# One state operand per chunk for both heads, and a common place modulo 256 bytes

## The chip, the cores and the metric

The kernel runs on one core of a Trainium2 chip. The metric is device time in microseconds (us), here that of the one core. The core has a matrix engine (PE, whose weight loads the profile lists apart as PEld), a vector engine (DVE), a scalar engine (ACT), GpSimd (POOL) and a queue engine (SP) that issues most transfers. Every engine takes its own instructions in the order in which they stand.

## The reference, cut to what matters

One layer of a decoder trunk over 1024 tokens of 1024 channels: a token mixer with three branches (causal pooling, RWKV-7 time mixing, attention into 256 memory tokens), then a gated feed-forward block with a short convolution. The change lies in the RWKV-7 branch, 16 heads of 64 channels, whose core is

```python
def step(state, inp):
    rt, wt, kt, vt, an, bn = inp
    sa = jnp.einsum('bhvk,bhk->bhv', state, an)
    state = state * wt[:, :, None, :] + sa[..., None] * bn[:, :, None, :] + vt[..., None] * kt[:, :, None, :]
    yt = jnp.einsum('bhvk,bhk->bhv', state, rt)
    return state, yt
```

It starts from a zero state and gives `yt` for each of 1024 tokens. Around it stand the input projection `z = h @ w_in`, the gates, the output projections and the feed-forward products; all are float32.

## The kernel before, in words

Activations lie channel-major: 128 channels over the partitions, the tokens along the free axis. A large product is made in float32r from operands split in a high and a low part: per 128 rows of weights there are three matmuls of 128x512 (`mm3`, L167 high weights by high data, L168 high by low, L169 low by high). The projections of `h` read `hh`/`hl` as the moving side and weight tiles `whi`/`wlo` as the stationary side; POOL and ACT make `whi`/`wlo` from a raw tile.

The recurrence runs in 4 groups (`rwkv_group`), each of 4 heads: two pairs `i` of two heads, one head of a pair on partitions 0 to 63 (`lo`), the other on 64 to 127 (`up`). The tokens are cut into 16 chunks of 64. A group has three parts:

- **Chunk products** (L542 to L559), for all chunks at once: per chunk the stationary `BK` (64 rows, 128 columns: the two key-like operands of one head) meets `AR`, 128 moving columns, once for `lo` (L549) and once for `up` (L556). The banks `ps` are masked by DVE into `NT` and `AR`, and ACT copies the outputs' part to `RB`. Transposes (`pt`) and products of values (`pv`, `pbo`) stand among them.
- **Inversion** of a triangular matrix per chunk on DVE (L584 to L600), while PE works through projections (`fill_to`), then two rows of 32x32 products (`pz`, `pw`).
- **Scan** (L645 to L693), chunk after chunk. `visit` (L636) chains matmuls in an order written out: remainders `pr` (four float32 matmuls), DVE copies them to `Rs`, `pu` applies `NT`, DVE and ACT copy `pu` to `HV`, `ph` and `py` make the next state and the output, DVE adds the decayed state into `HV` of the next chunk.

[...] Matmuls with fewer than 128 rows or columns use a part of the array; the profile writes rows*columns, such as `128*64`, and two that use different columns run side by side.

A scheduler that is given the dependencies and the written-out chains sets each engine's final order and puts projection matmuls between the visits; tiles that need no certain place are laid out by pools in the order in which they are made. The program therefore fixes, for each tile, a place in its partition. Places modulo 256 bytes of the two sides of the 128x512 float32r matmuls, from the built program before (after the change both are 224 for all of these):

| moving | stationary | matmuls | which |
|---|---|---|---|
| 224 | 192 | 3776 | `hh`/`hl`, the feed-forward's first half `h2h`/`h2l`, `yh`/`yl`, `mgl` by `whi`/`wlo` |
| 64 | 192 | 640 | `oh`, `ol`, `ph_`, `pl_`, `mgh` by `whi`/`wlo` |
| 224 or 64 | 64 or 224 (unequal) | 648 | a part of `psf`, the up products with weights `wt` |
| equal | equal | 1656 | `psd` (876, `f` by `u`, both at 64), the rest of `psf` (780) |

Of the kernel before, what the change touches and what calls it, by code (L numbers as in the profile page):

```python
# [9 lines left out]
F32 = mybir.dt.float32  # L10
# [7 lines left out]
P = 128  # L18
T = 1024
# [25 lines left out]
def trunk_kernel(ctx: ExitStack, tc: tile.TileContext, xT, memT, pvec, w_in, w_kv, w_upd, w_upg,  # L45
# [59 lines left out]
                        base=-1, channel_multiplier=-1)  # L105
    G.memset(smask, 1.0)
    G.memset(smask.rearrange("p (c s) -> p c s", s=C)[:, :, 0:1], 0.0)
    eps = const.tile([P, 3], F32, name="eps")
    for j, e in enumerate((NORM_EPS, L2_EPS, LNX_EPS)):
        G.memset(eps[:, j:j + 1], e)  # L110
# [226 lines left out]

    def up_tiles():
        return (wp.tile([P, 2, P], F32, name="uraw", tag="wraw0", bufs=3),
                wp.tile([P, 2, P], FR, name="uhi", tag="uhi", bufs=2),  # L340
                wp.tile([P, P], FR, name="ulo", tag="ulo", bufs=1))

    def load_up(ap):
        raw, hi, lo = up_tiles()
        raw, hi = raw[:, 0], hi[:, 0]
        SP.dma_start(raw, ap)
        split_w(raw, hi, lo)
        return hi, lo
# [6 lines left out]
    def load_up2(ap):  # L355


        raw, hi, _ = up_tiles()
# [72 lines left out]

    def rwkv_group(g, kv):
        tagA, tagB, tagC = ([f"X{i}{(g + n) % 3}" for i in range(2)] for n in range(3))
        AR = rw.tile([P, 2, 3, T], F32, name="AR", tag="AR")
        Dc = rw.tile([P, 2, NCH], F32, name="Dc", tag="Dc")
        tBN = [rw.tile([P, 2, T], F32, name=f"tBN{i}", tag=tagC[i]) for i in range(2)]
        tHV = rw.tile([P, 2, 2, T], F32, name="tHV", tag="HV")
# [1 line left out]
        def c3(ap):  # L439
            return ap.rearrange("p (c s) -> p c s", s=C)  # L440
# [16 lines left out]
        vs = []  # L457
        turn = [0]

        def product_bank(name):  # L460

            turn[0] = (turn[0] + 1) % 3
            shape = [P, 4, 2, C]
            return pss.tile(shape, F32, name=name, tag="s") if turn[0] else \
                psk.tile(shape, F32, name=name, tag="k")

        for i in range(2):
            p = 2 * g + i
            t0_, t1_ = kv[i][:, 0], kv[i][:, 1]
            t2_, t3_ = tBN[i][:, 0], tBN[i][:, 1]  # L470
            t4_, t5_ = tHV[:, i, 0], tHV[:, i, 1]
            r_ = AR[:, i, 1]
# [12 lines left out]
            in_block(8 + p, shifted(p, r_))  # L485

            dst = c3(AR[:, i, 0])
# [51 lines left out]
        for i in range(2):  # L539
            us = slice(NCH * i, NCH * i + NCH)  # L540
            for c0 in range(0, NCH, 4):
                def bc(m, q):  # L542
                    return m[q].unsqueeze(1).broadcast_to([64, 4, C])
                cs = slice(c0, c0 + 4)
                lo, up = slice(0, 64), slice(64, 128)
                ps = product_bank("ps1")
                for c in range(4):
                    t = slice((c0 + c) * C, (c0 + c + 1) * C)
                    PE.matmul(ps[:, c], BK[i][lo, c0 + c], AR[lo, i, 0:2, t], start=True, stop=True)  # L549
                A.copy(RB[i][:, 0, cs], ps[:, :, 1])  # L550
                V.tensor_tensor(NT[lo, i, cs], ps[lo, :, 0], bc(mstrict, lo), op=ALU.mult)
                V.tensor_tensor(c3(AR[up, i, 0])[:, cs], ps[up, :, 0], bc(mstrict, up), op=ALU.mult)
                ps = product_bank("ps2")
                for c in range(4):
                    t = slice((c0 + c) * C, (c0 + c + 1) * C)
                    PE.matmul(ps[:, c], BK[i][up, c0 + c], AR[up, i, 1:3, t], start=True, stop=True)  # L556
                A.copy(RB[i][:, 1, cs], ps[:, :, 0])
                V.tensor_tensor(NT[up, i, cs], ps[up, :, 1], bc(mstrict, up), op=ALU.mult)
                V.tensor_tensor(c3(AR[lo, i, 2])[:, cs], ps[lo, :, 1], bc(mstrict, lo), op=ALU.mult)  # L559
            for b in range(2 if i == 0 else 0):  # L560
                bonus(b)

# [40 lines left out]
        for u0 in (0, 16):  # L603
# [11 lines left out]
                for q0, q1 in ends:  # L615
                    PE.matmul(ps[q0, u], Z[q1, u0 + u], NTu[q1, u0 + u, 32:64], start=True, stop=True)
            for q0, q1 in ends:
                A.copy(NTu[q0, us, 32:64], ps[q0])


        for i in range(2):
# [2 lines left out]
                                op=ALU.mult)  # L624


        lo, up = slice(0, 64), slice(64, 128)
# [4 lines left out]
        def bank(name):  # L632
            turn[0] ^= 1
            return (psc if turn[0] else psk).tile([P, 2, C], F32, name=name, tag="c" if turn[0] else "k")

        def visit(products, after):  # L636

# [8 lines left out]
        for c in range(NCH):  # L646
            t = slice(c * C, (c + 1) * C)
            once = dict(start=True, stop=True)
            pr = bank("pr")
            py = pss.tile([P, 2, C], F32, name="py", tag="s")  # L650
            ke, ko = (up, lo) if c == 0 else (slice(0, P), slice(0, P))
            row = []
            for i in range(2):
# [4 lines left out]
            made = V.tensor_copy(Rs, pr).ins  # L658
            pu = bank("pu")
            row = []  # L660
# [5 lines left out]
            visit(row, made if c else None)  # L666
# [13 lines left out]
            if c + 1 < NCH:  # L680
# [5 lines left out]
                if c + 2 < NCH:  # L686
# [6 lines left out]
            A.copy(AR[:, :, 1, t], py)  # L693

        for i in range(2):
            p = 2 * g + i
            y = AR[:, i, 1]
# [149 lines left out]
    for hd in range(4):  # L849
        for t0, _ in HALVES:  # L850
# [7 lines left out]
            for u in range(2):  # L858
                ps = psg.tile([P, 2, 256], F32, name="psco", tag="g0")
                for tt in range(2):  # L860
                    ts_ = slice((2 * u + tt) * P, (2 * u + tt + 1) * P)
                    mm3(ps[:, tt], (qh[:, ts_], ql[:, ts_]), (kh[:, hd], kl[:, hd]), True, True)
                mx = as_.tile([P, 8], F32, name="mxs", tag="mxs", bufs=2)
# [745 lines left out]
```

## Time and profile before

| what | value |
|---|---|
| median of 3 runs | 2084.89 us (2083.38 to 2085.0) |
| the profiled execution's own time | 2084.65 us |
| its span, first to last instruction | 2082.7 us |
| mean granted PE clock | 0.993 |
| PE records | 12246 |
| stretches with chunk products (first to last) | 131.4 to 843.7 us |
| stretches of the scans | 237.0 to 968.2 us |
| up products `psf` | 1508.4 to 1845.0 us |
| down products `psd` | 1848.1 to 2056.6 us |

A row of the timeline gives start and length in us, engine, line, operation, `output<-inputs`, the part of the array (`rows*columns`), the shape, and how many equal records were merged. In a dense stream the distance from one record's start to the next is what a matmul costs; its listed length also holds the time in which its end drains while the next runs.

### The profile page before, as it was taken

To read this page: it belongs to the slowest core of one execution; us is meant where nothing else is said; L and a number is where in the kernel's file an instruction comes from. 1 tells how busy PE (TensorE), PEld (TensorE's weight loads), DVE (VectorE), ACT (ScalarE), POOL (GpSimd) and SP (SyncE) were. 2 spreads that over 40 slices of the span, in tenths; PEclk is the share of its full clock that TensorE was granted. 3 is DMA by queue.
4 is the path that set the end of the run, shared out by engine and by line. 5 is a ranking of instruction groups with operands and counts; after the bars stand their busy time and mean duration, and the time that the engine had idled before them with its cause. 6 is when DMAs were issued, how large, how long until landed. Compare 5 with 4: busy or idle time off the path is not lost.

```text
span 2082.7 us, 34125 instructions
## 1 busy us (share of the span) xinstructions
PE 2026.5 (97%) x12246; PEld 1559.1 (75%) x12246; DVE 1358.2 (65%) x2167; ACT 1070.6 (51%) x2252; POOL 810.8 (39%) x917
## 2 busy tenths in 40 slices
PE   8999999999999999999999999998999999999997
PEld 5777767776778667876878878776778877777886
DVE  6567437664667357833795452769877777777798
ACT  7585348623772368434566243545443444444644
POOL 5521213121222121212122355565578888842341
PEclk9999999999999999999999999999999999999999
DMA  4312211120212021213526443634222222169766
GB/s 155 129 41 74 67 51 67 67 82 22 87 61 89 30 92 44 86 55 120 172 84 223 129 134 107 220 102 151 94 88 83 82 78 76 61 185 273 168 178 152
DMA packets 176713, 221.83 MB, mean 107 GB/s; under 512 B 16544, under 2 KB 128288, under 8 KB 176544
## 3 DMA queue, kind: packets, MB, share of 16 engines
q1 hardware_dynamic: 163616, 204.44, 30.2%
q0 software_dynamic: 11856, 14.16, 4.2%
q8 instruction: 97, 1.59, 0.3%
q10 hardware_dynamic: 1072, 1.05, 0.1%
q14 instruction: 72, 0.59, 0.1%
HBM read 170.30 MB, written 49.28 MB: 105 GB/s over the span
## 4 chain that ended last, share of the span: by engine, by line
PE 36%; DVE 5%; DMA 4%; POOL 3%; issue 2%; ACT 2%; SPq 1%; POOLq 0%; ACTq 0%; DVEq 0%
PE psg L167 6%; PE psg L169 6%; PE psg L168 6%; PE psf L169 3%; PE psf L167 3%; PE psf L168 3%; POOL wt L1027 2%; PE psd L168 2%; PE psd L169 2%; PE psd L167 2%; DMA R<-d_f 1%; POOL sm L1012 1%; DMA a<-in_w_fup 1%; ACT d L1043 1%; DMA fw<-in_w_fdn 1%
## 5 line engine op out<-in xcount | busy, mean ns | idle before, releaser
L131 POOL TENSOR_TENSOR wlo<-wraw,whi 128x256 fp32r<-128x256 f32 x472 | 410.4, 878 | 951.7 <-ACT whi L128 760.2
L167 PE MATMUL psg<-hh,whi 128*128 128x512 f32 x928 | 383.6, 413 | 2.5 <-DVE kv L314 2.5
L169 PE MATMUL psg<-hh,wlo 128*128 128x512 f32 x928 | 379.8, 409 | 0.1
L168 PE MATMUL psg<-hl,whi 128*128 128x512 f32 x928 | 378.8, 408 | 0.0
L128 ACT CAST whi<-wraw 128x256 fp32r<-128x256 f32 x472 | 182.7, 403 | 227.9 <-PE psg L168 122.1
L167 PEld LDWEIGHTS psg<-hh,whi 128*128 128x128 f32 x928 | 174.6, 188 | 46.5 <-DVE kv L314 3.8
L169 PEld LDWEIGHTS psg<-hh,wlo 128*128 128x128 f32 x928 | 174.3, 188 | 45.9 <-POOL wlo L131 5.1
L168 PEld LDWEIGHTS psg<-hl,whi 128*128 128x128 f32 x928 | 174.7, 188 | 42.9 <-issue 3.6
L1027 POOL TENSOR_TENSOR wt<-a,wt 128x256 fp32r<-128x256 f32 x136 | 133.8, 1012 | 30.8 <-ACT wt L1026 30.8
L167 PE MATMUL psd<-f,u 128*128 128x512 f32 x292 | 115.0, 394 | 5.7 <-ACT f L1347 3.4
L168 PE MATMUL psd<-f,u 128*128 128x512 f32 x292 | 115.0, 394 | 1.0 <-DVE f L1351 1.0
L169 PE MATMUL psd<-f,u 128*128 128x512 f32 x292 | 114.3, 393 | 0.4 <-DVE u L1351 0.4
L1027 POOL TENSOR_TENSOR wt<-sm,wt 128x256 fp32r<-128x256 f32 x102 | 106.8, 1067 | 14.6 <-ACT wt L1026 14.6
L169 PE MATMUL psf<-h2h,wt 128*128 128x512 f32 x272 | 108.0, 397 | 0.4 <-POOL wt L1027 0.3
L168 PE MATMUL psf<-h2l,wt 128*128 128x512 f32 x272 | 107.0, 393 | 0.0
L167 PE MATMUL psf<-h2h,wt 128*128 128x512 f32 x272 | 106.8, 393 | 0.0
L1026 ACT CAST wt<-sm 128x256 fp32r<-128x256 f32 x102 | 37.9, 404 | 128.2 <-POOL sm L1012 124.2
L1045 DVE SCALAR_TENSOR_TENSOR d<-z,pv,d 128x1023 f32<-128x1023 f32 x68 | 91.6, 1347 | 12.0 <-ACT d L1043 9.5
L169 PE MATMUL psf<-t,wt 128*128 128x512 f32 x204 | 81.3, 399 | 1.9 <-POOL wt L1027 1.9
L168 PE MATMUL psf<-t,wt 128*128 128x512 f32 x204 | 80.3, 394 | 0.0
L167 PE MATMUL psf<-t,wt 128*128 128x512 f32 x204 | 80.2, 393 | 0.0
L685 DVE TENSOR_TENSOR HV<-ph,Hd 64x128 f32<-64x128 f32 x112 | 32.3, 289 | 71.8 <-PE ph L639 47.7
(422 smaller groups left out, 4751.3 us busy)
## 6 DMA issues: line engine op xcount, KB each, us to landing
wraw<-in_w_in SPq DMA_DIRECT2D x240, 128.0 KB, 2.3
a<-in_w_fup SPq DMA_DIRECT2D x128, 128.0 KB, 2.4
d_zg<-st SPq DMA_DIRECT2D x48, 256.0 KB, 2.7
wraw<-in_w_fup SPq DMA_DIRECT2D x80, 128.0 KB, 2.4
fw<-in_w_fdn SPq DMA_DIRECT2D x33, 256.0 KB, 4.5
fraw<-d_f SPq DMA_DIRECT2D x33, 256.0 KB, 5.2
wraw<-in_w_prwkv SPq DMA_DIRECT2D x64, 128.0 KB, 2.4
wraw<-in_w_o SPq DMA_DIRECT2D x64, 128.0 KB, 2.5
```

What stands on the lines that cost most here:

```text
L128: last_whi[0] = A.copy(hi, src).ins
L131: (V if lo_on_dve[0] else G).tensor_tensor(lo, src, hi.bitcast(F32), op=ALU.subtract)
L167: first = PE.matmul(ps, wh, xh, start=start, stop=False)
L168: PE.matmul(ps, wh, xl, start=False, stop=False)
L169: last_mm[0] = PE.matmul(ps, wl, xh, start=False, stop=stop).ins
L685: ready = V.tensor_tensor(HV[q, :, c + 1, e], ph[q], Hd[q], op=ALU.add).ins
L1012: eng.tensor_tensor(out_[u], a[u], b[u], op=op)
L1026: A.copy(w[0][:, us], src[u])
L1027: last_low[0] = G.tensor_tensor(w[1][:, us], src[u], w[0][:, us].bitcast(F32), op=ALU.subtract).ins
L1043: A.activation(d, z, AF.Identity, scale=col("cw2", j), bias=col("cb", j))
L1045: V.scalar_tensor_tensor(d[:, n:], z[:, :T - n], col(cw, j), d[:, n:], op0=ALU.mult, op1=ALU.add)
```

## The change

**One operand.** `AR` keeps its size, but is now cut into `A2`, which per chunk holds two blocks of 64 columns side by side (`e` = 0, 1), and `RY`, the receptance and later the output. For the `lo` head block 0 is set and block 1 starts at zero, for the `up` head the other way round; POOL makes the zeros (L440 and L498 of the changed kernel). One matmul of 128 rows, 128 columns and 128 moving columns per chunk then gives the products of both heads, masked as before. The outputs' products (`RY`) are no longer part of it: they are matmuls of their own, 64 moving columns by the 128 columns of `BK`, one head and eight chunks per bank, chained one behind the other.

**Remainders.** `pr` is one matmul of 128x128 by 128 columns per pair instead of two of 128x64 by 64 columns; half of its output is not used. `Rs` is twice as wide. `HV` of the first chunk gets zeros so that its full height can be read. Within a chunk `pu` now stands ahead of the `py` products of the old state.

**Places.** A tile `cpad` of 32 bytes, eight `zc` instead of four, `mxs` of 32 columns instead of 8, and `ulo` moved from one pool to another shift the tiles behind them.

```diff
+    const.tile([P, 8], F32, name="cpad")
-        zc = wp.tile([P, 1], F32, name="zc", tag="zc", bufs=4)
+        zc = wp.tile([P, 1], F32, name="zc", tag="zc", bufs=8)
...
-        AR = rw.tile([P, 2, 3, T], F32, name="AR", tag="AR")
+        AR = rw.tile([P, 6 * T], F32, name="AR", tag="AR")
+        A2 = AR[:, :4 * T].rearrange("p (i c e s) -> p i c e s", i=2, e=2, s=C)
+        RY = AR[:, 4 * T:].rearrange("p (i t) -> p i t", i=2)
+        for i in range(2):
+            G.memset(A2[lo, i, :, 1], 0.0)
...
-            A.copy(AR[64:128, i, 2], AR[64:128, i, 0])
+            A.copy(A2[up, i, :, 1], A2[up, i, :, 0])
+            G.memset(A2[up, i, :, 0], 0.0)
...
-                    PE.matmul(ps[:, c], BK[i][lo, c0 + c], AR[lo, i, 0:2, t], start=True, stop=True)
-                A.copy(RB[i][:, 0, cs], ps[:, :, 1])
+                    PE.matmul(ps[:, c], BK[i][:, c0 + c], A2[:, i, c0 + c], start=True, stop=True)
...
-                    PE.matmul(ps[:, c], BK[i][up, c0 + c], AR[up, i, 1:3, t], start=True, stop=True)
-                A.copy(RB[i][:, 1, cs], ps[:, :, 0])
+            for e, q in enumerate((lo, up)):
+                for c0 in (0, 8):
+                    ps = psc.tile([P, 8, C], F32, name="ps2", tag="c") if e and c0 else \
+                        product_bank("ps2", 8, C)
+                    for c in range(8):
+                        m = PE.matmul(ps[:, c], BK[i][q, c0 + c], RY[q, i, t], start=True, stop=True)
+                        if after is not None:
+                            later(m, after)
+                        after = m.ins
+                    A.copy(RB[i][:, e, c0:c0 + 8], ps)
...
-                row.append(((pr[up, i], AR[ko, i, 2, t], HV[ko, i, c, 1]), once))
-                row.append(((pr[lo, i], AR[ke, i, 0, t], HV[ke, i, c, 0]), once))
-            visit(row, ready)
-            Rs = rw.tile([P, 2, C], F32, name="Rs", tag="Rs", bufs=1)
+            visit([((pr[:, i], A2[:, i, c], HV[:, i, c]), once) for i in range(2)], ready)
+            Rs = rw.tile([P, 2, 2, C], F32, name="Rs", tag="Rs", bufs=1)
...
+            row = [((pu[q, i], NT[q, i, c], Rs[q, i, e]), once) for i in range(2) for e, q in enumerate((lo, up))]
             for i in range(2 if c else 0):
-                row.append(((py[lo, i], HV[lo, i, c, 0], AR[lo, i, 1, t]), kw))
-                row.append(((py[up, i], HV[up, i, c, 1], AR[up, i, 1, t]), kw))
-            row += [((pu[q, i], NT[q, i, c], Rs[q, i]), once) for i in range(2) for q in (lo, up)]
+                row.append(((py[lo, i], HV[lo, i, c, 0], RY[lo, i, t]), kw))
+                row.append(((py[up, i], HV[up, i, c, 1], RY[up, i, t]), kw))
```

What this moves on PE, the engine that the prediction turns on. In the scan, one chunk of the first group before (`psg` is a projection matmul, the others are as named above; sizes are those of the output of one matmul):

```order
L639 MATMUL pr<-HV,AR 64x64 x4
L168 MATMUL psg<-hl,whi 128x512
L639 MATMUL py<-AR,HV 64x64 x4
L639 MATMUL pu<-Rs,NT 64x64 x4
L169 MATMUL psg<-hh,wlo 128x512
L167 MATMUL psg<-hh,whi 128x512
L168 MATMUL psg<-hl,whi 128x512
L169 MATMUL psg<-hh,wlo 128x512
L639 MATMUL ph<-HV,BKN_1344 64x64 x2
L639 MATMUL ph<-HV,BKN_1345 64x64 x2
L639 MATMUL py<-RB_1342,HV 64x64 x2
L639 MATMUL py<-RB_1343,HV 64x64 x2
```

and a chunk of the same group in the changed program, up to `ph` (the four `py` matmuls behind it stand as before):

```order
L652 MATMUL pr<-HV,AR 128x128 x2
L168 MATMUL psg<-hh,whi 128x512
L169 MATMUL psg<-hl,whi 128x512
L170 MATMUL psg<-hh,wlo 128x512
L652 MATMUL pu<-Rs,NT 64x64 x4
L652 MATMUL py<-AR,HV 64x64 x4
L168 MATMUL psg<-hh,whi 128x512
L169 MATMUL psg<-hl,whi 128x512
L170 MATMUL psg<-hh,wlo 128x512
L168 MATMUL psg<-hh,whi 128x512
L652 MATMUL ph<-HV,BKN_1347 64x64 x2
L652 MATMUL ph<-HV,BKN_1348 64x64 x2
```

The remainders are two full matmuls, three projection matmuls instead of one stand between them and `pu`, and `pu` has passed `py`. With the two projection matmuls behind the last `py`, which both have, a chunk now holds 9 of them instead of 7; the number in the whole program is the same.

In the chunk products of the second group, before (L549 and L556 are the two heads' products):

```order
L549 MATMUL ps_3540<-AR,BK_3174 128x128 x4
L556 MATMUL ps_3580<-AR,BK_3174 128x128
L556 MATMUL ps_3548<-AR,BK_3174 128x128 x4
L556 MATMUL ps_3580<-AR,BK_3174 128x128
L556 MATMUL ps_3564<-AR,BK_3174 128x128 x4
L556 MATMUL ps_3580<-AR,BK_3174 128x128
L168 MATMUL psg<-hl,whi 128x512
L549 MATMUL ps_3572<-AR,BK_3174 128x128 x4
L169 MATMUL psg<-hh,wlo 128x512
L549 MATMUL ps_3588<-AR,BK_3174 128x128 x4
```

and now (L554 is the product of both heads, L566 the outputs' product):

```order
L554 MATMUL ps_3548<-AR,BK_3173 128x128 x4
L170 MATMUL psg<-hh,wlo 128x512
L168 MATMUL psg<-hh,whi 128x512
L169 MATMUL psg<-hl,whi 128x512
L554 MATMUL ps_3566<-AR,BK_3173 128x128 x4
L170 MATMUL psg<-hh,wlo 128x512
L168 MATMUL psg<-hh,whi 128x512
L169 MATMUL psg<-hl,whi 128x512
L566 MATMUL ps_3575<-AR,BK_3173 128x64 x8
L566 MATMUL ps_3585<-AR,BK_3173 128x64 x8
L566 MATMUL ps_3595<-AR,BK_3173 128x64 x8
L566 MATMUL ps_3605<-AR,BK_3173 128x64 x8
```

Of 256 chunk products with 128 moving columns 128 are left, and 256 with 64 moving columns are new, in runs of 8 to 32. Counted over the whole PE order, two neighbours use the array cut in different ways 572 times before and 376 times now: of the 196 that are gone 128 lie around `pr`, 64 around the chunk products (96 before, 32 now), 4 elsewhere.

More of the change, by code (lines that the diff above doesn't have):

```diff
@@ L339, in up_tiles @@
         return (wp.tile([P, 2, P], F32, name="uraw", tag="wraw0", bufs=3),
-                wp.tile([P, 2, P], FR, name="uhi", tag="uhi", bufs=2),
-                wp.tile([P, P], FR, name="ulo", tag="ulo", bufs=1))
+                wp.tile([P, 2, P], FR, name="uhi", tag="uhi", bufs=2))
     def load_up(ap):
-        raw, hi, lo = up_tiles()
+        raw, hi = up_tiles()
         raw, hi = raw[:, 0], hi[:, 0]
+        lo = pz.tile([P, P], FR, name="ulo", tag="ulo", bufs=1)
         SP.dma_start(raw, ap)
@@ L355, in load_up2 @@
     def load_up2(ap):
-        raw, hi, _ = up_tiles()
+        raw, hi = up_tiles()
         lo = ulo2
@@ L433, in rwkv_group @@
         tagA, tagB, tagC = ([f"X{i}{(g + n) % 3}" for i in range(2)] for n in range(3))
[L434 removed]
+        AR = rw.tile([P, 6 * T], F32, name="AR", tag="AR")
+        A2 = AR[:, :4 * T].rearrange("p (i c e s) -> p i c e s", i=2, e=2, s=C)
+        RY = AR[:, 4 * T:].rearrange("p (i t) -> p i t", i=2)
+        lo, up = slice(0, 64), slice(64, 128)
+        for i in range(2):
+            G.memset(A2[lo, i, :, 1], 0.0)
         Dc = rw.tile([P, 2, NCH], F32, name="Dc", tag="Dc")
@@ L458, in rwkv_group, with product_bank @@
         turn = [0]
-        def product_bank(name):
+        def product_bank(name, *shape):
             turn[0] = (turn[0] + 1) % 3
-            shape = [P, 4, 2, C]
+            shape = [P, *shape]
             return pss.tile(shape, F32, name=name, tag="s") if turn[0] else \
@@ L471, in rwkv_group @@
             t4_, t5_ = tHV[:, i, 0], tHV[:, i, 1]
-            r_ = AR[:, i, 1]
+            r_ = RY[:, i]
             BK = BKs[i]
@@ L485, in rwkv_group @@
             in_block(8 + p, shifted(p, r_))
-            dst = c3(AR[:, i, 0])
+            dst = A2[:, i, :, 0]
             V.scalar_tensor_tensor(dst[:, :, 1:], c3(t5_)[:, :, 1:], -1.0, c3(t3_)[:, :, :C - 1],
@@ L544, in rwkv_group @@
                 cs = slice(c0, c0 + 4)
-                lo, up = slice(0, 64), slice(64, 128)
-                ps = product_bank("ps1")
+                ps = product_bank("ps1", 4, 2, C)
                 for c in range(4):
-                    t = slice((c0 + c) * C, (c0 + c + 1) * C)
-                    PE.matmul(ps[:, c], BK[i][lo, c0 + c], AR[lo, i, 0:2, t], start=True, stop=True)
-                A.copy(RB[i][:, 0, cs], ps[:, :, 1])
+                    PE.matmul(ps[:, c], BK[i][:, c0 + c], A2[:, i, c0 + c], start=True, stop=True)
                 V.tensor_tensor(NT[lo, i, cs], ps[lo, :, 0], bc(mstrict, lo), op=ALU.mult)
[L552 to L556, printed above, removed]
-                A.copy(RB[i][:, 1, cs], ps[:, :, 0])
-                V.tensor_tensor(NT[up, i, cs], ps[up, :, 1], bc(mstrict, up), op=ALU.mult)
-                V.tensor_tensor(c3(AR[lo, i, 2])[:, cs], ps[lo, :, 1], bc(mstrict, lo), op=ALU.mult)
+                V.tensor_tensor(A2[up, i, cs, 0], ps[up, :, 0], bc(mstrict, up), op=ALU.mult)
+                V.tensor_tensor(NT[up, i, cs], ps[up, :, 1], bc(mstrict, up), op=ALU.mult)
+                V.tensor_tensor(A2[lo, i, cs, 1], ps[lo, :, 1], bc(mstrict, lo), op=ALU.mult)
+            after = None
+            for e, q in enumerate((lo, up)):
[3 more added lines that the diff above has]
+                    for c in range(8):
+                        t = slice((c0 + c) * C, (c0 + c + 1) * C)
+                        m = PE.matmul(ps[:, c], BK[i][q, c0 + c], RY[q, i, t], start=True, stop=True)
[3 more added lines that the diff above has]
+                    A.copy(RB[i][:, e, c0:c0 + 8], ps)
             for b in range(2 if i == 0 else 0):
@@ L617, in rwkv_group @@
             for q0, q1 in ends:
-                A.copy(NTu[q0, us, 32:64], ps[q0])
+                solved = A.copy(NTu[q0, us, 32:64], ps[q0]).ins
         for i in range(2):
@@ L630, in rwkv_group, with bank @@
         turn = [0]
-        def bank(name):
+        def bank(name, *shape):
             turn[0] ^= 1
-            return (psc if turn[0] else psk).tile([P, 2, C], F32, name=name, tag="c" if turn[0] else "k")
+            return (psc if turn[0] else psk).tile([P, 2, *shape, C], F32, name=name, tag="c" if turn[0] else "k")
+        V.memset(HV[lo, :, 0, 0], 0.0)
+        V.memset(HV[up, :, 0, 1], 0.0)
         def visit(products, after):
@@ L648, in rwkv_group @@
             once = dict(start=True, stop=True)
-            pr = bank("pr")
+            pr = bank("pr", 2)
             py = pss.tile([P, 2, C], F32, name="py", tag="s")
-            ke, ko = (up, lo) if c == 0 else (slice(0, P), slice(0, P))
-            row = []
-            for i in range(2):
-                row.append(((pr[up, i], AR[ko, i, 2, t], HV[ko, i, c, 1]), once))
-                row.append(((pr[lo, i], AR[ke, i, 0, t], HV[ke, i, c, 0]), once))
-            visit(row, ready)
-            Rs = rw.tile([P, 2, C], F32, name="Rs", tag="Rs", bufs=1)
+            visit([((pr[:, i], A2[:, i, c], HV[:, i, c]), once) for i in range(2)], ready)
+            Rs = rw.tile([P, 2, 2, C], F32, name="Rs", tag="Rs", bufs=1)
             made = V.tensor_copy(Rs, pr).ins
             pu = bank("pu")
-            row = []
+            row = [((pu[q, i], NT[q, i, c], Rs[q, i, e]), once) for i in range(2) for e, q in enumerate((lo, up))]
             for i in range(2 if c else 0):
                 kw = dict(start=i == 0, stop=False)
-                row.append(((py[lo, i], HV[lo, i, c, 0], AR[lo, i, 1, t]), kw))
-                row.append(((py[up, i], HV[up, i, c, 1], AR[up, i, 1, t]), kw))
-            row += [((pu[q, i], NT[q, i, c], Rs[q, i]), once) for i in range(2) for q in (lo, up)]
-            visit(row, made if c else None)
+                row.append(((py[lo, i], HV[lo, i, c, 0], RY[lo, i, t]), kw))
+                row.append(((py[up, i], HV[up, i, c, 1], RY[up, i, t]), kw))
+            visit(row, made if c else solved)
             V.tensor_copy(HV[lo, :, c, 0], pu[lo])
@@ L692, in rwkv_group @@
                         A.activation(Hd[:, i], Hn[:, i], AF.Identity, scale=Dc[:, i, c + 1:c + 2])
-            A.copy(AR[:, :, 1, t], py)
+            A.copy(RY[:, :, t], py)
         for i in range(2):
             p = 2 * g + i
-            y = AR[:, i, 1]
+            y = RY[:, i]
             gt = rw.tile([P, 2, T], F32, name="gt", tag=tagA[i])
@@ L862, in trunk_kernel @@
                     mm3(ps[:, tt], (qh[:, ts_], ql[:, ts_]), (kh[:, hd], kl[:, hd]), True, True)
-                mx = as_.tile([P, 8], F32, name="mxs", tag="mxs", bufs=2)
+                mx = as_.tile([P, 32], F32, name="mxs", tag="mxs", bufs=2)
                 V.reduce_max(mx[:, 0:2], ps, axis=AX.X)
```

1 line of the change is left out of this document (removed).

## The prediction

> **What bounds the kernel now.** I read the page first, then PE's waits.
>
> ```profile
> PE 2026.5 (97%) x12246; PEld 1559.1 (75%) x12246; DVE 1358.2 (65%) x2167; ACT 1070.6 (51%) x2252; POOL 810.8 (39%) x917
> PEclk9999999999999999999999999999999999999999
> PE psn L1096 <- DVE s L1091: 8.3, 1, 8.3
> PE psf L169 <- POOL wt L1027: 2.3, 9, 0.4
> PE pr L639 <- DVE HV L685: 0.3, 1, 0.3
> ```
>
> PE is busy 97% of the span at a full granted clock, and its longest wait for another engine is 8.3 us. So the time is what PE's records cost, one behind the other, and I cost the change in distances from start to start on PE. The last row, one wait for `HV` in 64 chunks, will prove too kind. One chunk of the first scan, from PE's timeline, and behind it the group of all late `py`:
>
> ```profile
> 253.63 0.45 PE L639 MATMUL pr<-HV,AR 128*64 128x64 f32 x8
> 254.01 0.49 PE L167 MATMUL psg<-hh,whi 128*128 128x512 f32 x1
> 254.44 0.45 PE L639 MATMUL py<-AR,HV 64*64 64x64 f32 x8
> 254.72 0.40 PE L639 MATMUL pu<-Rs,NT 64*64 64x64 f32 x8
> 255.05 0.50 PE L168 MATMUL psg<-hl,whi 128*128 128x512 f32 x1
> 255.38 0.39 PE L169 MATMUL psg<-hh,wlo 128*128 128x512 f32 x1
> 255.61 0.40 PE L167 MATMUL psg<-hh,whi 128*128 128x512 f32 x1
> 255.85 0.39 PE L168 MATMUL psg<-hl,whi 128*128 128x512 f32 x1
> 256.17 0.45 PE L639 MATMUL ph<-HV,BKN 128*64 128x64 f32 x8
> 256.45 0.40 PE L639 MATMUL py<-RB,HV 128*64 128x64 f32 x8
> 256.78 0.50 PE L169 MATMUL psg<-hh,wlo 128*128 128x512 f32 x1
> 257.12 0.40 PE L167 MATMUL psg<-hh,whi 128*128 128x512 f32 x1
> 257.49 0.45 PE L639 MATMUL pr<-HV,AR 128*64 128x64 f32 x8
> L639 PE MATMUL py<-RB,HV x512: 221/222/271, 248.8 to 968.2; 128*64 128x64 f32 x171
> ```
>
> The reader is to see that a matmul of the full array takes 0.23 us beside its like (255.38 to 255.61), but 0.32 to 0.43 where a neighbour cuts the array in another way. Eight `py` records last 0.40 us together and one lasts 0.222; two run side by side, so three steps of pairs take 0.178: 0.059 us a pair. The chunk takes 257.49 - 253.63 = 3.86 us: 7 projection matmuls at 0.233 (below) are 1.63, 20 pairs 1.18, and 1.05 is left for 6 changes of cut, 0.174 us each.
>
> **Term 1, places.** Two dense streams of one shape, each with its first and last row (210 and 466 steps), and two products of 12 matmuls out of one stage:
>
> ```profile
> 407.33 0.40 PE L169 MATMUL psg<-hh,wlo 128*128 128x512 f32 x1
> 456.33 0.39 PE L169 MATMUL psg<-hh,wlo 128*128 128x512 f32 x1
> 1925.26 0.40 PE L169 MATMUL psd<-f,u 128*128 128x512 f32 x1
> 2030.91 0.39 PE L167 MATMUL psd<-f,u 128*128 128x512 f32 x1
> 1519.62 0.39 PE L167 MATMUL psf<-t,wt 128*128 128x512 f32 x1
> 1522.11 0.39 PE L169 MATMUL psf<-t,wt 128*128 128x512 f32 x1
> 1525.71 0.39 PE L167 MATMUL psf<-h2h,wt 128*128 128x512 f32 x1
> 1528.28 0.39 PE L169 MATMUL psf<-h2h,wt 128*128 128x512 f32 x1
> ```
>
> `psg` (places 224 and 192) takes 49.00/210 = 233.3 ns, `psd` (64 and 64) 105.65/466 = 226.7. That could be the stage. But inside one stage the same two values stand side by side: the product at 1519.62 has both sides at 224 and takes 2.49/11 = 226 ns, the one at 1525.71 has moving 224 and weights 64 and takes 2.57/11 = 234. So the distance goes with the relative place, and I take it as the cause. Afterwards all places are equal. 3776 + 648 unequal matmuls at 6.6 ns are 29.2 us; the 640 with 64 against 192, whose streams I did not find dense, I take at 5 ns, 3.2 us. Together 32, the upper bound of the gain; the lower is 0, if the stage sets it. Not all arrives: half of the 4.3 us in `psf` goes into the waits for POOL's `wt`, some 1 us lies in the shadow of the 8.3 us wait, 2 more under short waits at the start and between groups. I take **-27 us**; nothing in these rows lets it be a loss.
>
> **Term 2, the scan.** `pr` becomes 4 records with 128 weight and 128 moving columns. Their price is at least a pair's 0.059 us; the nearest row is the chunk product with as many columns on both sides, 0.112 us a record (next part), and I take that. `pr` then costs 0.448 instead of 4 x 0.059 = 0.236, +0.21 us, and two changes of cut go, -0.35: -0.14 us a chunk, -8.9 in 64 chunks, and 4 changes elsewhere -0.7. On PE alone -9.6 us (-23 at 0.059).
>
> But `pr` is bound to DVE. The state behind the `ph` above, the remainders behind the last `pr` above, and a copy of 512 columns:
>
> ```profile
> 256.74 0.61 DVE L685 TENSOR_TENSOR HV<-ph,Hd 64x128 f32<-64x128 f32 x2 [1.29 <-ACT whi L128]
> 257.98 0.29 DVE L658 COPY Rs<-pr 128x128 f32<-128x128 f32 x1 [0.31 <-PE pr L639]
> L1116 DVE COPY o<-psg x16: 678/692/694, 1250.2 to 1384.0; 128x512 f32<-128x512 f32 x16
> ```
>
> `HV` is complete at 257.35, and `pr` starts 0.14 us later, at 257.49, as closely as one engine follows another here. So `pr` waits for `HV` already, though the view of waits hardly says so: from `ph` to `pr` the chain needs 1.32 us. Afterwards PE has less to do there: 0.61 for `ph` and `py` (256.17 to 256.78), 0.34 and 0.23 for two projection matmuls, no change of cut, 1.18. So 0.14 us of waiting shows in each of the 60 chunks that have a predecessor, +8.4, and the gain in place of those two matmuls, 13 ns, is lost too, +0.8. Bounds: 0, should the projections between them cover it all, and 15, should the chain also grow by 0.1.
>
> On the other side `Rs` doubles to 256 columns: between 0.29 us (128) and 0.69 (512), by proportion 0.42. It starts when `pr` has drained (three steps 0.336, one record 0.272, 0.04 to DVE: 0.65), ends at 1.07, and `pu` can follow 0.14 later, at 1.21. PE has `pr`, three projection matmuls and a change of cut ahead of `pu`: 0.448 + 0.68 + 0.17 = 1.30. That hides it with 0.09 us to spare; with the cover gone, each 0.1 us would cost 6. `pu` ahead of the old state's `py` makes `pu` earlier, and nothing waits for that `py`. I count 1 us for chunks in which `Rs` finds DVE busy. The term: -9.6 + 8.4 + 0.8 + 1 = **+0.6 us**: what the joint remainders save on PE, PE spends waiting.
>
> **Term 3, chunk products.** PE's timeline, the groups of the chunk products and of the two loads' forms, and two loads that follow one another:
>
> ```profile
> 378.50 0.49 PE L168 MATMUL psg<-hl,whi 128*128 128x512 f32 x1
> 378.92 1.16 PE L549 MATMUL ps<-AR,BK 64*128 64x128 f32 x8
> 380.00 0.50 PE L169 MATMUL psg<-hh,wlo 128*128 128x512 f32 x1
> 382.10 0.72 PE L556 MATMUL ps<-AR,BK 64*128 64x128 f32 x5
> L549 PE MATMUL ps<-AR,BK x256: 272/272/374, 131.4 to 841.0; 64*128 64x128 f32 x128
> L549 PEld LDWEIGHTS ps<-AR,BK x256: 182/188/189, 131.4 to 840.9; 64*128 64x128 f32 x128
> L639 PEld LDWEIGHTS pu<-Rs,NT x512: 129/135/136, 241.6 to 966.9; 64*64 64x64 f32 x171
> 249.15 0.19 PEld L167 LDWEIGHTS psg<-hh,whi 128*128 128x128 f32 x1
> 249.26 0.19 PEld L168 LDWEIGHTS psg<-hl,whi 128*128 128x128 f32 x1
> ```
>
> Five records last 0.72 us and one 0.272, so 0.112 us each. A projection matmul and eight records take 1.50 us: 0.233 + 0.896, and 0.37 for two changes, 0.186 each. Before: 512 records, 57.3 us, less an estimated 5 where the two heads alternate and run side by side, and 96 changes, 17.9: 70.2 us. After: 256 records of the joint product (full array) at 0.112, 28.7; 32 changes, 6.0; and 512 records of the outputs' product with 64 moving columns. What one of these costs the trace does not show. At least 0.059 us, if the moving columns set it as in the pairs; at most 0.112, if the weights do, since these are the same 128 columns of `BK`. A load lasts 188 ns for 128 columns and 135 for 64, and the loads at 249.15 and 249.26 stand 0.11 apart although both are of the same kind: a load of 128 columns seems to hold its path for 0.11 us. I take that, 0.110: 56.3 us, together 91.0, **+21 us** (-5 at 0.059).
>
> [...]
>
> POOL gets 16 fills of 64x1024 and ACT larger copies; PE has projections to do meanwhile, and POOL is busy 39%. Without that cover a fill ahead of a joint product would cost 1.4 us by the pace of the 512 columns above, an estimate, 8 times: 11 us.
>
> **The sum:** 2084.65 - 27 + 0.6 + 21 = 2079.3, told as 2079 us. The profiled execution is 0.2 us under the median, so no correction.
>
> **Rivals.** *The outputs' products stream at 0.059 us:* 26 us less, 2053. For it, a short moving side; against it, the two loads 0.11 apart. *The place is not what sets 233 ns in the projections:* another part of the stage does, and only `psf` gains, 2 us: 2084.65 - 2 + 0.6 + 21 = 2104, slower. It decides from the point at which the projections gain under 3 ns a matmul: 11 us of gain then stand against 21.6. For it: no equal pair in the groups' stage runs undisturbed; against it, both `psf` rows. [...] *The scan's chain grows:* `Rs` of twice the width is late by a further 0.12 us, where the first load after a stall lies open: +7, 2086, no change; for it the cover of 0.09. *The scan hides its wait:* the projections move into the gap, and PE keeps its 9.6 us: 2070. That the change would not do what it says is excluded by the order and the places.
>
> **How the numbers follow.** The forecast, 2079, has 0.48, its own range 2073 to 2086 (4 us of term 1, 3 of each other). Streaming 0.10, places without effect 0.16, the longer chain 0.16, the hidden wait 0.10. A measurement tells 0.2%, 4.2 us, from no change. Faster (under 2080.7): 0.32 of the forecast, 0.10, 0.10 and 0.02 of the chain: 0.54. Same: 0.14 of the forecast, 0.07 of the chain: 0.21. Slower: 0.02, 0.07 and the 0.16 of the places: 0.25. The range is 2056 to 2095: it leaves out most of streaming and of the places, and takes in the rest.
>
> **What would show it.** A dense run of `psg` at 227 ns instead of 233 (term 1). `pr` as four records 0.112 us apart, and from `ph` to `pr` still 1.32 us, so that the chunk with nine projection matmuls takes 3.86 + 2 x 0.227 = 4.31 us less some 0.05; without the wait it would be 4.13 (term 2). Outputs' products 0.11 apart, not 0.06 (term 3). It is wrong if `psg` stays at 233 ns, if PE waits for `Rs` at `pu`, or if `ph` to `pr` shrinks.

## The result

The changed kernel is slower by 1.8%: 2120.89 us (2119.2 to 2125.47, 4 runs) against 2084.14 us, a ratio of 1.0182 with a 95% interval of 1.0171 to 1.0194. The forecast was 2079 us, with a range of 2056 to 2095. The profiled execution took 2119.66 us; its span is 2117.9 us, its mean granted clock 0.978 where the kernel before had 0.993.

The page after, first PE's share and then its granted clock in 40 slices:

```profile
PE 2057.2 (97%) x12246; PEld 1613.4 (76%) x12246; DVE 1366.6 (65%) x2175; ACT 1066.3 (50%) x2220; POOL 828.7 (39%) x933
PEclk9998999899999999899999999999999999999999
```

PE has the same number of records and the same share, and yet the span is 35 us longer. Three slices of the clock row show 8, and these lie in the chunk products of three of the four groups. Cut finer, in windows of 4 us around the first of them (columns: window, length, PE's busy time and records, granted clock, DMA share, GB/s):

```profile
156.00:160.00 4.00, 4.00 (x42) 1.00 0.11 37
160.00:164.00 4.00, 4.00 (x21) 0.50 0.00 0
164.00:168.00 4.00, 4.00 (x8) 0.50 0.00 0
168.00:172.00 4.00, 4.00 (x15) 0.72 0.28 111
172.00:176.00 4.00, 4.00 (x30) 1.00 0.37 147
184.00:188.00 4.00, 4.00 (x29) 0.91 0.02 4
188.00:192.00 4.00, 4.00 (x20) 0.50 0.00 0
```

PE is busy for all of each window, and the clock halves twice. PE's timeline of the changed kernel says under what:

```profile
155.42 9.02 PE L566 MATMUL ps<-AR,BK 64*128 64x64 f32 x64
164.37 3.78 PE L520 MATMUL pbo<-kv,bonesr 128*128 128x512 f32 x4
173.80 1.97 PE L566 MATMUL ps<-AR,BK 64*128 64x64 f32 x16
186.48 6.36 PE L566 MATMUL ps<-AR,BK 64*128 64x64 f32 x32
...
200.28 0.39 PE L168 MATMUL psg<-hh,whi 128*128 128x512 f32 x1
204.82 0.39 PE L170 MATMUL psg<-hh,wlo 128*128 128x512 f32 x1
```

The rows of L566 are the outputs' products. Every float32 matmul has left two records (x512 in the trace for these 256 matmuls, x8 for the four `pr` matmuls of a chunk before), and runs are counted in records from here on. Sixteen in a row take 1.97 us at a full clock, 0.112 us apart. Within the runs of 64 and of 32 the distance changes from 0.112 to 0.213 us and stays there to the end of the run, and what comes next pays as well (`pbo`, 0.85 us from start to start behind the run, 0.43 at a full clock later in the same stage). It is so in all four groups: a run of 64 takes 8.4 to 10.5 us where 7.2 would do, a run of 32 takes 4.0 to 6.4 where 3.6 would. The clock that was missing in the eight falls, length times the missing half, sums to 30.7 us. The kernel before has no such fall between its first and its last chunk product.

The last two rows are one of the dense streams of projections, 20 steps apart: 4.54/20 = 227 ns, where the kernel before had 233. So term 1's mechanism is there, and something else cost more than it gave.

### The profile page after: what moved, and what is told of

Same layout as the page of the kernel before. It is cut to its first block, busy times and chain, and to the rows that moved or that the text cites. A ratio compares the mean times of both kernels' runs of the same rounds, so it can differ in the third digit from the quotient of the medians.

```text
span 2117.9 us, 34184 instructions
## 1 busy us (share of the span) xinstructions
PE 2057.2 (97%) x12246; PEld 1613.4 (76%) x12246; DVE 1366.6 (65%) x2175; ACT 1066.3 (50%) x2220; POOL 828.7 (39%) x933
## 4 chain that ended last, share of the span: by engine, by line
PE 64%; DVE 11%; ACT 8%; POOL 6%; DMA 5%; issue 5%; SPq 0%; POOLq 0%; ACTq 0%; DVEq 0%
PE psg L169 13%; PE psg L168 13%; PE psg L170 13%; PE ps L566 3%; POOL wt L1034 3%; PE psd L169 2%; PE psd L168 2%; PE psd L170 2%; PE pr L652 2%; DMA a<-in_w_fup 2%; POOL sm L1019 2%; PE ps L554 2%; ACT d L1050 1%; PE py L652 1%; PE pu L652 1%
## 5 line engine op out<-in xcount | busy, mean ns | idle before, releaser
L132 POOL TENSOR_TENSOR wlo<-wraw,whi 128x256 fp32r<-128x256 f32 x472 | 418.6, 896 | 948.3 <-ACT whi L129 868.8
```

The lines of the kernel that those rows point to most:

```text
L132: (V if lo_on_dve[0] else G).tensor_tensor(lo, src, hi.bitcast(F32), op=ALU.subtract)
```

## Experiments

Theory G: the places bring their gain, the remainders nothing, and the loss is the clock, which falls while long runs of the outputs' products keep PE busy and do little. Its rivals: P, that equal places make PE denser and the clock falls for that; and, on what counts as little, the share of the time in which columns stream (G1) or the unused half of the rows and the length of the run (G2). Ratios below are against the kernel before on the same chip. Three chips were used: on the first (pads alone, 128 columns, all rows, one bank) the kernel before took 2080.4 us, on the second (the changed kernel again, the remainders, one addition, the kernel before again) 2079.1, on the third (the last two kernels) 2079.4. Times from different chips are compared by their ratios.

**The pads alone**, on the kernel before:

```diff
+    const.tile([P, 8], F32, name="cpad")
-        zc = wp.tile([P, 1], F32, name="zc", tag="zc", bufs=4)
+        zc = wp.tile([P, 1], F32, name="zc", tag="zc", bufs=8)
...
+        lo = pz.tile([P, P], FR, name="ulo", tag="ulo", bufs=1)
-                mx = as_.tile([P, 8], F32, name="mxs", tag="mxs", bufs=2)
+                mx = as_.tile([P, 32], F32, name="mxs", tag="mxs", bufs=2)
```

> The kernel before with the pads alone: all places of the 128x512 float32r matmuls at 224, chunk products and scan as before. Theory G (the loss comes from the outputs' chunk products, whose long runs let the granted clock fall to 0.50; the places do what was forecast): 2084 - 27 = 2057 us, 2052 to 2064, psg 227 ns apart, no fall of the clock in the stretch of the chunk products. Rival P (equal places make PE denser, and that brings the falls of the clock): falls to 0.50 appear in the groups, and the time is 2075 to 2090.

Measured: 2071.0 us, 0.9958 (0.9943 to 0.9973): 8.7 us faster, 5.6 to 11.9. No fall of the clock in the chunk products (granted 1.00 in 150 to 200 us), so P is out. But only a third of the forecast gain arrived. Its median is the lowest of this study.

**128 moving columns** in the outputs' products of the changed kernel, everything else as it was:

```diff
-                        m = PE.matmul(ps[:, c], BK[i][q, c0 + c], RY[q, i, t], start=True, stop=True)
+                        m = PE.matmul(ps[:, c:min(c + 2, 8)], BK[i][q, c0 + c],
+                                      RY[q, i, t.start:t.start + C * min(2, 8 - c)], start=True, stop=True)
```

> The changed kernel, with the outputs' products given 128 moving columns instead of 64 (each but the last of a bank also writes the next chunk's place, which the next product then overwrites, so the outputs stay the same). Same order, same weights, same 128x64 part of the array used per head. Theory G1 (the clock falls because 64 columns stream for too small a share of the 112 ns that the weight load takes): twice the stream at 0.112 us a record still, no falls to 0.50 in the groups, 2121 - 31 = 2090 us (2084 to 2098). Rival G2 (what counts is that half of the rows is unused, or the length of the runs): falls as before, 2115 to 2125.

**All 128 rows** in them, 64 moving columns:

```diff
-                        m = PE.matmul(ps[:, c], BK[i][q, c0 + c], RY[q, i, t], start=True, stop=True)
+                        m = PE.matmul(ps[:, c], BK[i][:, c0 + c], RY[:, i, t], start=True, stop=True)
```

> The changed kernel, with the outputs' products taken over all 128 rows instead of one head's 64, still with 64 moving columns; they then add up both heads, which changes what is computed in the outputs. Theory G1 (share of streaming): falls to 0.50 in all four groups as before, 2115 to 2125 us. Rival G2 (unused rows): no falls, about 2090.

Measured: 2089.61 us (1.0049, 1.0031 to 1.0066) and 2085.5 us (1.0026, 1.0013 to 1.0039). One row of PE's timeline and one window of each, first 128 columns, then 128 rows:

```profile
154.90 7.02 PE L566 MATMUL ps<-AR,BK 64*128 64x128 f32 x64
150.00:200.00 50.00, 49.59 (x316) 1.00 0.16 59
```

```profile
154.98 7.25 PE L566 MATMUL ps<-AR,BK 128*128 128x64 f32 x64
150.00:200.00 50.00, 50.00 (x317) 1.00 0.16 59
```

Twice the moving columns in the same run of 64, mostly at the same 0.112 us a record: no fall. Twice the rows with the short stream: no fall either, so G1 as I had put it is wrong, and so is G2. Either doubling is enough: with a record every 0.112 us, 64 rows by 64 moving columns let the clock fall, 64 by 128 and 128 by 64 do not. That the clock follows the product of rows and columns would fit, but it is not shown.

**One bank** for all outputs' products, so that each 16 records wait for ACT's copy and other matmuls come between:

```diff
-                    ps = psc.tile([P, 8, C], F32, name="ps2", tag="c") if e and c0 else \
-                        product_bank("ps2", 8, C)
+                    ps = psk.tile([P, 8, C], F32, name="ps2", tag="k")
```

> The changed kernel, with all outputs' products in one PSUM bank, so that each 16 records wait for ACT's copy and the order puts other matmuls between: runs of at most 16 of them, where there were runs of 64 and 32. Theory G (the length of a run in which PE streams little): few or no falls to 0.50, 2121 - 31 = 2090 us, up to 2100 with waits for the copies. Rival P (pads): falls stay wherever psg is dense, 2115 to 2125.

Measured: 2093.59 us, 1.0070 (1.0054 to 1.0087), no fall in the groups' chunk products. One window, with the busy time of PE, PEld, DVE, ACT and POOL ahead of the clock:

```profile
150.00:200.00 50.00, 50.00 (x327) 41.81 (x322) 34.54 (x71) 28.45 (x62) 5.96 (x8) 1.00 0.18 64
```

With the records as they were and their runs cut, the loss goes too. How long a run it takes can be worked out from the records of the clock. Within a trace all its changes lie on one grid with a step of 3.41 us. In the changed kernel (both profiled executions) and in this one, each of the 16 falls in the chunk products came at the end of a step in which the outputs' products had 0.72 to 1.00 of the time. Every other step there that began at a full clock had 0.67 or less, and the clock stayed at 1.00 behind it.

**The changed kernel again**, beside the others:

> The changed kernel itself, beside the others on one chip. Theory G: falls of the clock to 0.50 in all four groups, some 30 us above the kernel with 128 moving columns (about 2118 where the kernel before takes 2080).

Measured: 2116.9 us, 1.0181 (1.0164 to 1.0198), with falls in all four groups. Against the kernel with 128 columns that is 1.0181 - 1.0049 = 0.0132, 27.5 us, between 22 and 33 by the two intervals. This is what the falls cost, since at a full clock the records are 0.112 us apart in both kernels. The clock missing in the falls of this profile sums to 35.8 us, where it was 30.7 in the first: how long a fall lasts changes from execution to execution, and not all of it lengthens the kernel.

**The remainders as before**, on the kernel with 128 moving columns:

```diff
-            pr = bank("pr", 2)
+            pr = bank("pr")
...
-            visit([((pr[:, i], A2[:, i, c], HV[:, i, c]), once) for i in range(2)], ready)
-            Rs = rw.tile([P, 2, 2, C], F32, name="Rs", tag="Rs", bufs=1)
+            row = []
+            for i in range(2):
+                row.append(((pr[up, i], A2[:, i, c, 1], HV[:, i, c, 1]), once))
+                row.append(((pr[lo, i], A2[:, i, c, 0], HV[:, i, c, 0]), once))
+            visit(row, ready)
+            Rs = rw.tile([P, 2, C], F32, name="Rs", tag="Rs", bufs=1)
...
-            row = [((pu[q, i], NT[q, i, c], Rs[q, i, e]), once) for i in range(2) for e, q in enumerate((lo, up))]
+            row = [((pu[q, i], NT[q, i, c], Rs[q, i]), once) for i in range(2) for e, q in enumerate((lo, up))]
```

> The kernel with 128 moving columns in the outputs' products, and the remainders as before the change: four matmuls of 64x64 per chunk, Rs 128 columns wide; the order of everything else stays. Theory C (pr waits for the state, and PE's saving there is lost): the same time as with joint remainders, within 3 us; ph to pr stays 1.32 us. Rival (PE alone sets the scan): 9 to 10 us slower than with joint remainders, and ph to pr grows.

**One addition** for the state instead of two, also on the kernel with 128 moving columns (the upper heads' place, which then gets no state, is set to zero for all chunks):

```diff
-        V.memset(HV[up, :, 0, 1], 0.0)
+        V.memset(HV[up, :, :, 1], 0.0)
...
-                for q, e in ((lo, 0), (up, 1)):
...
-                        ready = V.tensor_tensor(HV[q, :, c + 1, e], ph[q], Hd[q], op=ALU.add).ins
...
+                    ready = V.tensor_tensor(HV[:, :, c + 1, 0], ph, Hd, op=ALU.add).ins
```

> The kernel with 128 moving columns in the outputs' products, with one DVE operation over 128 partitions in place of the two that complete the state HV; the upper heads' state then goes to the wrong place, which changes what is computed. The chain from ph to pr is 0.29 us shorter. The order then puts one projection matmul instead of two between py and pr. Theory C: pr comes earlier, ph to pr falls to about 1.03 us, and the time by 3 to 9 us. Rival (the chain does not bind): ph to pr falls only by the matmul that moved, and the time stays within 2 us.

Measured: 2088.37 us (1.0039, 1.0024 to 1.0054) for the old remainders and 2083.38 us (1.0020, 1.0010 to 1.0029) for one addition. Starts within a chunk, medians over the chunks of the commonest form, in ns, worked out from the traces:

```
                              pr to ph   ph to next pr   chunk   psg in a chunk
kernel before                 2537       1324            3861    7
128 columns, joint pr         3046       1325            4371    9
128 columns, old pr           3020       1327            4347    9
128 columns, one addition     3037        956            3993    8
```

With four small matmuls or two full ones, with 0.24 or 0.45 us of PE's time in `pr`, a chunk takes the same within 0.03 us, and `ph` to `pr` is 1.32 to 1.33 us: the way over DVE sets it. Against joint remainders the old ones are 0.0010 faster, 2 us, with an interval of -7 to +3 us, where the rival wanted them 9 to 10 us slower. When the way over DVE has one addition instead of two, `pr` comes 0.37 us earlier; 0.23 of this is the one projection matmul that now stands there instead of two, the other 0.14 was waiting. The time falls by 0.0029, 6 us (2 to 10). Theory C holds. In the changed kernel itself the two ends can be read, DVE's row ahead of PE's:

```profile
277.93 0.61 DVE L692 TENSOR_TENSOR HV<-ph,Hd 64x128 f32<-64x128 f32 x2 [1.33 <-PE ph L652]
279.41 0.42 DVE L666 COPY Rs<-pr 128x256 f32<-128x256 f32 x1 [0.54 <-PE pr L652]
```

```profile
278.69 0.68 PE L652 MATMUL pr<-HV,AR 128*128 128x128 f32 x4
279.13 0.48 PE L170 MATMUL psg<-hh,wlo 128*128 128x512 f32 x1
280.00 0.45 PE L652 MATMUL pu<-Rs,NT 64*64 64x64 f32 x8
```

`HV` ends at 278.54, `pr` starts 0.15 us later; `Rs` ends at 279.83, `pu` starts 0.17 later.

**Where the places' gain went.** The kernel before, profiled again, to set beside the pads alone. It ran on the second chip and the pads on the first, where the kernel before took 1.3 us more:

> The kernel before, for a profile on the same chip. Expected: the time of the kernel before within 0.2%, and a span within 5 us of the first profile's 2082.7.

Measured: 2078.51 us (0.9997, 0.9987 to 1.0008), span 2077.1 against 2067.3 us with the pads. All matmuls of `psg`, `psf` and `psd` in the two traces, by their place in an unbroken run of the same product; the distance is that to the next start, and one of over 245 ns is counted as disturbed (a wait, or a change of cut behind it). Worked out from the traces:

```
                                  count   undisturbed, ns      disturbed, us in all   all, us
                                          before   pads        before   pads          change
psg, first four and last of a run  1146   232.1    232.3      225.8    227.9         + 1.5
psg, later in a run                3342   233.0    227.0       23.8     33.3         -13.4
psf                                1428   230.9    227.6       18.5     29.9         + 0.4
psd                                 876   227.2    227.0       15.9     18.6         + 1.2
```

Where the gain exists it is 6.0 ns, close to the 6.6 of the forecast. It does not show in the first four matmuls of a run, and 1146 of the 4488 are such or the last of a run; in the scan's chunks all are. One run in the scan with equal places, in PE's timeline of the pads alone:

```profile
256.48 0.50 PE L170 MATMUL psg<-hh,wlo 128*128 128x512 f32 x1
256.82 0.40 PE L168 MATMUL psg<-hh,whi 128*128 128x512 f32 x1
257.06 0.40 PE L169 MATMUL psg<-hl,whi 128*128 128x512 f32 x1
257.29 0.40 PE L170 MATMUL psg<-hh,wlo 128*128 128x512 f32 x1
257.62 0.45 PE L640 MATMUL ph<-HV,BKN 128*64 128x64 f32 x8
```

The steps are 0.34, 0.24 and 0.23, as with unequal places (255.05 to 255.85 in the prediction's chunk). And where PE is faster, it waits longer for the weights. The waits of the weight load in `psf` (us in total, times, longest), in the kernel before and with the pads:

```profile
PEld psf L169 <- POOL wt L1027: 9.8, 21, 0.7
```

```profile
PEld psf L170 <- POOL wt L1028: 16.0, 34, 0.7
```

Two more kernels take a single pad away from the pads alone. Without the eight `zc`, the 3776 matmuls are equal, 640 (`oh`/`ol` and the like) and 648 of `psf` are not:

```diff
-        zc = wp.tile([P, 1], F32, name="zc", tag="zc", bufs=8)
+        zc = wp.tile([P, 1], F32, name="zc", tag="zc", bufs=4)
```

> The kernel before with all pads but the eight zc: the 3776 matmuls by whi and wlo that lay at 224 and 192 have equal places, 640 more and 648 of the up products stay unequal. Theory W (in psf the gain of equal places goes into waits for POOL's weights): psf costs what it costs with all pads, and only the 640 lose 2 to 4 us: 0.997 to 0.999 of the kernel before. Rival (each matmul's gain arrives): 648 and 640 matmuls at 6 ns, 7 to 8 us more than with all pads: 0.9995 of it.

Without `cpad`, the 3776 are unequal, the 640 equal:

```diff
-    const.tile([P, 8], F32, name="cpad")
```

> The kernel before with all pads but cpad: the 3776 matmuls by whi and wlo stay unequal (224 and 192), the 640 others are equal. Theory W: nearly all of the pads' 9 us came from the 3776, and 2 to 4 us from the 640: 0.998 to 1.000 of the kernel before, dense psg at 233 ns. Rival (the pads gain in another way, by what they move in memory): 0.996 as with all pads.

Measured: 2072.78 us, 0.9967 (0.9955 to 0.9979), and 2076.95 us, 0.9994 (0.9985 to 1.0004). The first is what theory W gives. `psf` takes 340.0 us with 648 unequal matmuls, 339.4 with none and 339.0 in the kernel before: the up products gain nothing from their places. POOL's pace fits as the reason: with the 648 unequal again the waits for `wt` are back at 11.2 us, from 16.0. What the 640 bring, 0.0009, is within the noise. With the 3776 unequal nearly all of the gain is gone, and their distance in dense streams is 233.3 ns again (227.2 where they are equal), so what the pads bring comes from the places and not from what else they move.

## Why the prediction was wrong

Steps, from the ratios times 2080 us:

| step | forecast, us | measured, us |
|---|---|---|
| term 1, places (pads alone) | -27 | -8.7 (-11.9 to -5.6) |
| terms 2 and 3 (128 columns, less pads alone) | +21.6 | +18.9 (14 to 24) |
| granted clock (changed, less 128 columns) | not in the sum | +27.5 (22 to 33) |
| together | -5 | +37.7 |

**The step that failed is term 3's price for the outputs' products.** "I take that, 0.110" was right for a record (0.112, decided between the bounds for the weights' side), and the joint products cost what was forecast: at the distances of a full clock all chunk products of the changed kernel come to some 86 us, against 66 before, +20, where +21 was forecast. What was missing is that this price holds at a full granted clock alone (at one half it is 0.213): the order shown ahead of the prediction has these records in runs of up to 64, up to 7.2 us of half the rows and half the moving columns, and the falls there cost 27.5 us that stand in no term. I read the clock as a constant; "at a full granted clock" in the first part is where the mistake entered. A 9 in the row of the clock only says 90% or more, and the mean stood in the table ahead of the prediction as 0.993: the clock was not 1.00 everywhere in the kernel before. Here are windows of its trace around its longest wait:

```profile
1405.00:1415.00 10.00, 10.00 (x44) 1.00 0.56 187
1415.00:1418.00 3.00, 0.08 (x1) 1.00 0.51 153
1418.00:1430.00 12.00, 6.60 (x16) 0.57 0.65 203
```

and PE there:

```profile
1414.69 0.39 PE L169 MATMUL psg<-h2h,wlo 128*128 128x512 f32 x1
1423.40 2.08 PE L1096 MATMUL psn<-s,ones 128*128 128x512 f32 x2 [8.32 <-DVE s L1091]
...
1427.83 0.63 PE L167 MATMUL psg<-h2h,whi 128*128 128x512 f32 x1
1428.26 0.63 PE L168 MATMUL psg<-h2l,whi 128*128 128x512 f32 x1
```

Here the clock went to one half 3.6 us after PE's last record had ended (at 1415.08), and stayed there for 10.2 us: matmuls over 4 us behind the wait still stand 0.43 us apart, against 0.23 ahead of it. The same half, for 10.2, 6.8 or 3.4 us, came with the outputs' products without any wait: from 156 to 164 us of the changed kernel PE and its weight loads are both busy for all of the 8 us. The eight falls there last one, two or three steps of 3.41 us, with records 0.213 us apart instead of 0.112, and cost 1.7, 3.4 or 5.1 us of clock each. A rival with the right sign could have stood in the prediction: eight falls of up to 10.2 us, the length of the one in the kernel before, at half speed are up to 41 us.

**Term 1** had the right mechanism and nearly the right size for a matmul (6.0 ns of 6.6), and was mis-sized in what arrives: 27 us were taken of 32, 8.7 came. Not seen was that a run's first four matmuls gain nothing, and that the gain in `psf` goes whole into waits, not half. By the rows of the table, 3342 matmuls at 6.0 ns are 20.0 us and 1388 of `psf` at 3.3 ns 4.6; of these 24.6 us 14.3 come off again: 6.6 in more and longer gaps inside the dense `psg` streams, 5.0 in `psf`, 1.2 in `psd` and 1.5 at the ends of runs. 10.3 are left between these two profiles. What the gaps inside the `psg` streams wait for was not traced.

**Term 2** held. The joint remainders bring nothing that can be told from noise: a ratio of 1.0049 against 1.0039 with the old ones, +2 us (-3 to +7), forecast +0.6. `ph` to `pr` stayed at 1.32 us, as predicted. The chunk takes 4.37 us where 4.26 was forecast; 0.06 of the 0.11 is that nine matmuls in short runs do not gain from their places, and the rest is open.

**The rivals.** Streaming at 0.059 is out (0.112). Places without effect in the projections is out for dense streams. The point from which that rival was to decide, 3 ns a matmul, was passed by the distance and not by the time: over 4424 matmuls, 8.7 us are 2 ns each. The hidden wait and the longer chain are out. None of the rivals held the mechanism that decided.

**Left open:** where the point lies between 64 rows by 64 columns and twice that; whether rows and columns weigh alike; and why equal places need some four matmuls to act.

## What to carry to other kernels

Before a long run of small matmuls is priced by its record, ask how few rows and columns it moves in 3 or 4 us: here a PE that was 100% busy with 64 rows by 64 columns lost half its clock (0.213 us a record instead of 0.112), and the `pbo` matmuls behind paid too (0.85 instead of 0.43 us). One way out was to break such runs with other matmuls, as one bank did (a ratio of 1.0070 against 1.0181), another to give them more columns or rows where the distance stayed at 0.112 us (1.0049 and 1.0026). And the 6.0 ns a matmul arrived here only from the fifth matmul of a run on, and not in the time of `psf`, where the weight loads then waited 16.0 us for POOL instead of 9.8; count the matmuls in dense streams and look who feeds them before multiplying.

## What the hardware showed that was not expected

The granted clock fell to 0.50 with PE busy without a gap: runs of 64-row matmuls with 64 moving columns, 0.112 us apart, halved it 2.9 to 5.3 us after a run of 64 began; with 128 rows or with 128 moving columns the same run at the same pace did not (1.00 from 150 to 200 us). The changes lay on a grid of 3.41 us; in the chunk products the 16 steps that ended in a fall had such records for 0.72 of their time or more, and no step that began at a full clock with 0.67 or less ended in one. Places modulo 256 bytes of the moving and the stationary side set the distance in the dense streams of float32r matmuls of 128x512 here; these are the distances over four kernels (the kernel before and the three with pads), from the fifth matmul of a run on, undisturbed, with the same places for six in a row (mean ns, with the count):

```
moving, stationary   apart   ns (count)
64, 64                 0     227.1 (843, psd)
96, 96                 0     227.0 (842, psd)
192, 192               0     227.2 (838, psd), 226.7 (373, psg)
224, 224               0     227.1 (3328, psg), 227.0 (837, psd)
224, 192              32     233.3 (2463, psg)
64, 192              128     233.3 (370, psg)
96, 224              128     232.4 (370, psg), 233.3 (201, psf)
64, 224              160     234.0 (203, psf)
224, 64              160     234.0 (264, psf)
```

In these rows it is the difference that counts, not the place: 226.7 to 227.2 ns at 0, whichever the place, and 232.4 to 234.0 at 32, 128 and 160. In the first four of a run and its last equal places brought nothing that shows (232.1 against 232.3 ns).
